# Two GpSimd products of each RWKV pair computed by VectorE, and the gate tile allocated from a longer-lived pool

## The chip, the cores and the metric

The kernel runs on one core of a Trainium2 chip. A core has five engines that run their own instruction queues side by side: TensorE (PE, matmuls; its weight loads are listed apart as PEld), VectorE (DVE), ScalarE (ACT), GpSimd (POOL) and SyncE (SP, which here only issues DMAs). They meet through semaphores: an instruction waits until the instructions that it depends on, on other engines or in DMA queues, have signalled. Within one engine the order is fixed, so an instruction that waits also holds up what stands behind it.

The metric is the device time of one launch in microseconds (us). The times shown are the median of several runs; the profile is of one execution.

## The reference

One layer of a hybrid trunk over 528 tokens (16 learned meta tokens ahead of 512), width 1024, all float32. Cut to what matters here:

```python
u = rmsnorm(h, norm_mix)
proj = u @ w_in                                     # 1024 -> RWKV, FoX and gate columns
gates = sigmoid(proj[..., C_RW + C_FX:] + b_gate)   # 2 x 1024 columns
y_rw = rwkv7_branch(...)                            # 8 heads of 64, delta rule over 64-token chunks
y_fx = fox_branch(...)                              # 8 heads, attention with forget gates
merged = gates[..., :1024] * (y_rw @ w_out_rw) + gates[..., 1024:] * (y_fx @ w_out_fx)
h = h + merged @ w_o
h = h + square(relu(rmsnorm(h) @ w_up)) @ w_down
```

In the RWKV branch, with `k`, `a`, `r` per head and `kk` the normalised key:

```python
k = k * (1.0 + (a - 1.0) * k_a)
y = wkv7_scan(r, decay, k, v, -kk, kk * a)
bonus = sum(r * k * r_k, axis=-1) * v
```

The changed products are two of these: `k` divided by the running decay of its chunk, and `r * k` for the bonus.

## The kernel before

Every float32 matrix product is made of three TensorE passes over a high and a low part (`hi`, `lo`) of each operand. For a weight block of 128x1024, SP loads two halves `wraw` of 128x512, ACT casts each to `whi` (L550), DVE subtracts to get `wlo` (L551), and PE runs `whi` with the high and low input and `wlo` with the high input (L582). In the later stages the same is done by `load_h` (L239 the load, L242 the casts).

The work goes through three stages:

- **Front** (0 to about 400 us): 40 projection blocks; the RWKV heads in four *pairs* (a pair is two heads side by side in the 128 partitions); the FoX attention; and the last 16 blocks, which are the gates. Pairs 0 and 1 form the first group, 2 and 3 the second; after a group's pairs come a triangular inverse and a chain over the 9 chunks of 64 tokens.
- **Merge** (about 400 to 460 us): eight rounds `m`. In each, two gate tiles `gl` come back from DRAM (L1261), ACT takes their tanh (L1262), PE makes two products `po` in PSUM banks with the tag `sm` (L1267, four banks, so two rounds), DVE multiplies gate and product (L1269), POOL adds the two (L1271), ACT and DVE write `mhi` and `mlo` (L1272, L1273). Then the product with `w_o`.
- **MLP** (to the end).

What sets the order. In the front, PE's order is written out by a planner: several generators run as streams, and `Turns.run` takes the stream of highest rank whose operands are ready by a clock of estimated times (`Clock.read`, L101 on, with `RATE` per engine). The other engines' orders are made by the framework's own scheduler from the program. In `Clock.read` an instruction is booked on the engine it runs on, except that `wlo` is booked as "Pool" (L116).

In a pair (`class Pair`) the steps that matter are these, all over 9 chunks of 64 columns (576, or 512 without the meta chunk):

- `keys`: from `okk` and the decay sum, PE makes the sums of squares `pkk`; L910 clamps them, ACT takes logarithm and exponential (L912, L913), L914 and L915 make the key `kp` (it lives in the tile `sg`), L916 normalises `okk`. Then L921 writes `KT`, L922 the first half of `BK`, **L923 the second half of `BK` as `kp3 * pinv` on POOL**, and L924 writes `KT` from all of `BK`.
- `rows`: L932, L933 and L935 on DVE write the tile `L` of the pair's first head, L934 and L938 on ACT copy its lower half to that of the second. **L939 writes `sq = orr * sg` on POOL**, the r·k product, which the PE product `pbn` of the bonus reads later.
- `scores`: in three rounds PE makes `psr` from `BK` and `L` (L964), DVE masks them into `Bm` and `L` (L965, L967), and PE transposes `KT` into `pbt` (L971). `psr` needs `BK` and both tiles `L`; `pbt` needs `KT`.

Between these, the same DVE queue carries the `wlo` subtractions (L551) and the token-shift evictions (L310: `orr`, `ov`, `okk`) of the projections, which PE also waits for; L636 and L638 make the forget gates, L225 and L1139 belong to the group norm and to the chain of chunks.

The 16 gate blocks go the way of `gate_job`: ACT evicts `pj` into `gt` (L595) and issues its store to the DRAM tile `gd` (L596) from its own queue. `gt` is one buffer of the pool `fp`, which lives for the front only; the tiles of the merge are taken from memory that the front's pools give back. The pool `wp`, with the weight tiles, is opened at L202 and lives through the whole kernel. Before the merge's first two rounds nothing but buffers holds the loads `gl` back: the gates `gd` 0, 1, 8 and 9 are in DRAM long before.

Of the kernel before, what the change touches and what calls it, by code (L numbers as in the profile page):

```python
# [9 lines left out]
F32 = mybir.dt.float32  # L10
# [4 lines left out]
ALU = mybir.AluOpType  # L15
# [6 lines left out]
S = 512  # L22
# [40 lines left out]
class Clock:  # L63
# [6 lines left out]
    def __init__(self, nc):  # L70
        self.nc = nc
        self.seen = len(nc.cur_bb.bb.instructions)
        self.pe = 0.0
        self.form = None
        self.urgent = False
        self.spans, self.w, self.r, self.free, self.rings = {}, {}, {}, {}, {}

    def last(self, name):
# [20 lines left out]
    def read(self):  # L99

        new = self.nc.cur_bb.bb.instructions[self.seen:]  # L101
        self.seen += len(new)
        for x in new:
            outs = [o.bass_ap for o in x.outs if hasattr(o, "bass_ap")]
            ins = [o.bass_ap for o in x.ins if hasattr(o, "bass_ap")]
            if not outs:
                continue
            for o in outs:
                t = o.tensor
                if hasattr(t, "cap_key") and t.name not in self.free:  # L110
                    ring, n = self.rings.setdefault(str(t.cap_key).rsplit("_", 2)[0], []), t.tag_meta.bufs
                    self.free[t.name] = self.last(ring[-n]) if len(ring) >= n else 0.0
                    ring.append(t.name)
            names = [a.tensor.name for a in ins]
            out = outs[0].tensor.name
            eng = "Pool" if out.startswith("wlo") else str(x.engine).split(".")[-1]  # L116

            def cols(a):
                return math.prod(n for _, n in a.ap[1:])
            deps = max([self.w.get(n, 0.0) for n in names] + [self.free.get(out, 0.0)])  # L120
            if eng == "PE":
                n = cols(outs[0])
                rows, width = x.tile_size
                if ins[0].dtype == F32R:
                    cost = n / 2400 + 0.013
                else:
                    cost = n / 600 * max(rows * width / 16384, 1 / 4)
                if self.form != tuple(x.tile_size):
                    self.form = tuple(x.tile_size)
                    cost += 0.1  # L130
                self.pe = end = max(self.pe, deps) + cost
            else:
                size = max([cols(a) for a in outs + (ins if "Reduce" in str(x.opcode) else [])])
                if eng in self.RATE and "DMA" not in str(x.opcode):
                    fixed, per = self.RATE[eng]
                    if eng == "DVE" and (getattr(x, "is_tensor_tensor_scan", False) or any(a.ap[-1][0] > 4 for a in outs + (ins[:1] if "Transpose" in str(x.opcode) else []))):
                        per *= 2
                    end = self.book(eng, max(deps, self.last(out)), fixed + per * size) + fixed + per * size
                else:
                    cost = 0.3 + size * 128 * 4 / 2.0e5  # L140
                    end = self.book("DMA", max(deps, self.last(out)), cost) + cost + 2.0
            for o in outs:
                self.w[o.tensor.name] = max(self.w.get(o.tensor.name, 0.0), end + self.HOP)
            for n in names:
                self.r[n] = max(self.r.get(n, 0.0), end + self.HOP)
# [44 lines left out]
def kernel(ctx, tc, ht, x, win, par, cst, gain, lora, wout, wo, wup, wdn, out, dbg=None):  # L190
# [4 lines left out]
    V, G, A = nc.vector, nc.gpsimd, nc.scalar  # L195
# [6 lines left out]
    wp = ctx.enter_context(tc.tile_pool(name="wp", bufs=2))  # L202
# [50 lines left out]
    def after(ins, prev):  # L253

        tc.add_manual_dep(ins.ins, prev.ins.name, mybir.DependencyInfo(mybir.DependencyClass.NoSync, mybir.DependencyReason.DATA),
                          reason="one accumulation at a time")
# [8 lines left out]
    def pinned(prev):  # L265

        if table["tanh"] or table["pin"] is None:
            p = nc.scalar.preload_act_table_set("natural_log_exp_and_others")
            after(p, prev)
            for x in table["tanh"]:  # L270
                after(p, x)
            table["tanh"], table["pin"] = [], p
        return table["pin"]
# [14 lines left out]
    with ExitStack() as st:  # L288
# [5 lines left out]
        def psm(name="psm"):  # L294
            return ps.tile([128, 512], F32, name=name, tag="sm", bufs=4)
# [22 lines left out]
        ck = Clock(nc)  # L318
# [180 lines left out]
        fp = st.enter_context(tc.tile_pool(name="fp", bufs=1))  # L499
# [7 lines left out]
        def banks(n):  # L507
            return ck.ring("sm", n, 4)
# [82 lines left out]
        def gate_job(i):  # L591
            def begin():
                def evac(po, sl):
                    gt = fp.tile([128, S], F32, name="gt")
                    act(gt, po, AF.Identity, bias=pr[:, C_BG + i:C_BG + i + 1])  # L595
                    A.dma_start(gates_d[i], gt)  # L596
                return evac
            return begin
# [226 lines left out]
        def v9(t):  # L825
            return t.rearrange("p (a b) -> p a b", b=64)
# [28 lines left out]
        class Pair:  # L855
# [44 lines left out]
            def keys(self):  # L900

                p = self.p
                okr, thr, kp, pinv = self.okk[:, PADT:], self.tha[:, PADT:], self.sg, v9(self.lc)
                self.sq = sq = rp.tile([128, TP], F32, name="sq")
                s_ = act(sq[:, :T], okr, AF.Square, scale=self.col(C_KK))
                yield lambda: max(ck.ready(sq), banks(2))
                for hc in (slice(0, HT), slice(HT, T)):
                    pq = psm("pkk")[:, :HT]
                    mm(pq, ones_blk, sq[:, hc], start=True, stop=True)
                    V.tensor_scalar(sq[:, hc], pq, 1e-24, None, ALU.max)  # L910
                pin = pinned(s_)
                after(act(sq[:, :T], sq[:, :T], AF.Ln), pin)  # L912
                act(sq[:, :T], sq[:, :T], AF.Exp, scale=-0.5)  # L913
                V.tensor_scalar(kp[:, PADT:], thr, prh[:, 2, p:p + 1], prh[:, 3, p:p + 1], ALU.mult, ALU.add)  # L914
                V.tensor_tensor(kp[:, PADT:], kp[:, PADT:], okr, ALU.mult)  # L915
                V.scalar_tensor_tensor(okr, okr, self.col(C_KK), sq[:, :T], ALU.mult, ALU.mult)  # L916
                kkn, kp3, tha3 = v9(self.okk), v9(kp), v9(self.tha)

                self.BK = BK = rp.tile([128, NCH, 2, 64], F32, name="BK", tag="BK")
                self.KT = KT = rp.tile([128, NCH, 2, 64], F32, name="KT", tag="KT")  # L920
                V.scalar_tensor_tensor(KT[:, :, 1, :], kkn, 0.5, pinv, ALU.mult, ALU.mult)  # L921
                V.scalar_tensor_tensor(BK[:, :, 0, :], tha3, 1.0, KT[:, :, 1, :], ALU.add, ALU.mult)  # L922
                G.tensor_tensor(BK[:, :, 1, :], kp3, pinv, ALU.mult)  # L923
                s_ = V.tensor_tensor(KT, BK, self.P[:, :, 63:64].unsqueeze(2).to_broadcast([128, NCH, 2, 64]), ALU.mult)  # L924
                if p == 0:
                    after(s_, low[0])

            def rows(self):

                kkn, r3, P = v9(self.okk), v9(self.orr), self.P  # L930
                self.L = l0, l1 = [kp.tile([128, NCH, 128], F32, name=f"L{e}", bufs=2) for e in range(2)]
                V.scalar_tensor_tensor(l0[:, :, 1:64], kkn[:, :, 1:64], -1.0, P[:, :, 0:63], ALU.mult, ALU.mult)  # L932
                V.tensor_scalar(l0[:, :, 0:1], kkn[:, :, 0:1], -1.0, None, ALU.mult)  # L933
                A.copy(l1[hss[1], :, :64], l0[hss[1], :, :64])  # L934
                s_ = V.tensor_tensor(l0[:, :, 64:128], r3, P, ALU.mult)  # L935
                if self.p == 0:
                    after(s_, low[0])
                A.copy(l1[hss[1], :, 64:], l0[hss[1], :, 64:])  # L938
                G.tensor_tensor(self.sq[:, :S], self.orr[:, 64:], self.sg[:, 64:], ALU.mult)  # L939
                self.rkb = rp.tile([128, 128], F32, name="rkb")  # L940
                after(V.tensor_scalar(self.rkb, ones_blk, self.col(C_RK), None, ALU.mult), last["DVE"])

# [673 lines left out]
```

## Time and profile before

| | |
|---|---|
| median of 3 runs | 826.9 us (826.32 to 827.44) |
| the profiled execution's own time | 826.71 us |
| its span in the trace | 824.9 us |
| mean granted TensorE clock | 0.998 |
| DVE busy | 607.8 us, 1196 instructions |
| ACT busy | 452.5 us, 941 instructions |
| POOL busy | 120.0 us, 124 instructions |
| POOL, L923 | 4 products 128x576, 1407, 1568 and 1801 ns (min, median, max) |
| POOL, L939 | 4 products 128x512, 1677, 1764 and 2303 ns |

The span is what the trace covers; the execution's own time has 1.8 us more around it. Times inside the trace are counted from the span's start. A row of a timeline gives start, duration, engine, line, operation, tiles and, in brackets, how long the engine was idle before it and what ended the wait. A row "x2" holds two instructions that followed one another. The four pairs run their L923 at 43, 74, 165 and 235 us and their L939 at 48, 81, 182 and 247 us.

### The profile page before, as it was taken

To read this page: it belongs to the slowest core of one execution; us is meant where nothing else is said; L and a number is where in the kernel's file an instruction comes from. 1 tells how busy PE (TensorE), PEld (TensorE's weight loads), DVE (VectorE), ACT (ScalarE), POOL (GpSimd) and SP (SyncE) were. 2 spreads that over 40 slices of the span, in tenths; PEclk is the share of its full clock that TensorE was granted. 3 is DMA by queue.
4 is the path that set the end of the run, shared out by engine and by line. 5 is a ranking of instruction groups with operands and counts; after the bars stand their busy time and mean duration, and the time that the engine had idled before them with its cause. 6 is when DMAs were issued, how large, how long until landed. Compare 5 with 4: busy or idle time off the path is not lost.

```text
span 824.9 us, 15506 instructions
## 1 busy us (share of the span) xinstructions
PE 808.1 (98%) x5886; PEld 667.3 (81%) x5886; DVE 607.8 (74%) x1196; ACT 452.5 (55%) x941; POOL 120.0 (15%) x124
## 2 busy tenths in 40 slices
PE   8999999998999999999999999999999999999998
PEld 6979887876987886778788889888888888888886
DVE  6797985687779855975267655875698678867988
ACT  7767548766575457664366534664445434543452
POOL 1021000010011000000022003100740174017400
PEclk9999999999999999999999999999999999999999
DMA  7222221211211311223687404533742365236532
GB/s 240 75 71 79 69 92 56 79 40 65 79 52 54 128 46 61 90 66 116 218 289 226 159 0 151 176 82 100 225 150 87 115 221 150 77 118 208 156 107 76
DMA packets 51483, 95.88 MB, mean 116 GB/s; under 512 B 5832, under 2 KB 7240, under 8 KB 51408
## 3 DMA queue, kind: packets, MB, share of 16 engines
q1 hardware_dynamic: 47680, 86.37, 33.0%
q0 software_dynamic: 1280, 4.20, 1.7%
q10 hardware_dynamic: 2448, 4.33, 1.5%
q8 instruction: 46, 0.75, 0.4%
q14 instruction: 29, 0.24, 0.1%
HBM read 88.56 MB, written 6.31 MB: 115 GB/s over the span
## 4 chain that ended last, share of the span: by engine, by line
PE 86%; DVE 5%; ACT 5%; issue 2%; DMA 1%; POOL 0%; DVEq 0%; ACTq 0%; SPq 0%
PE pj L582 22%; PE po L1357 21%; PE po L1484 12%; PE pd L1484 5%; PE po L1267 4%; PE po L1329 3%; PE pj L394 1%; PE pd L1298 1%; PE po L1298 1%; PE psc L751 1%; PE py L805 1%; PE psr L964 1%; PE ppt L788 1%; DVE wlo L551 1%; PE pch L1115 1%
## 5 line engine op out<-in xcount | busy, mean ns | idle before, releaser
L582 PE MATMUL pj<-uhi,whi 128*128 128x264 f32 (+1 forms) x480 | 164.3, 342 | 0.0
L582 PE MATMUL pj<-uhi,wlo 128*128 128x264 f32 (+1 forms) x480 | 153.9, 321 | 1.8 <-DVE wlo L551 1.8
L582 PE MATMUL pj<-ulo,whi 128*128 128x264 f32 (+1 forms) x480 | 153.8, 320 | 0.0
L242 DVE TENSOR_TENSOR wlo<-wraw,whi 128x512 fp32r<-128x512 f32 x84 | 81.0, 973 | 36.8 <-ACT whi L242 36.8
L582 PEld LDWEIGHTS pj<-uhi,whi 128*128 128x128 f32 x480 | 90.7, 189 | 12.9 <-issue 4.4
L582 PEld LDWEIGHTS pj<-uhi,wlo 128*128 128x128 f32 x480 | 90.7, 189 | 8.8 <-DVE wlo L551 2.2
L582 PEld LDWEIGHTS pj<-ulo,whi 128*128 128x128 f32 x480 | 91.0, 190 | 6.7 <-issue 1.6
L1357 PE MATMUL po<-zhi,whi 128*128 128x512 f32 (+1 forms) x248 | 94.8, 382 | 0.0
L1357 PE MATMUL po<-zlo,whi 128*128 128x512 f32 (+1 forms) x248 | 94.8, 382 | 0.0
L1357 PE MATMUL po<-zhi,wlo 128*128 128x512 f32 (+1 forms) x248 | 94.8, 382 | 0.0
L242 ACT CAST whi<-wraw 128x512 fp32r<-128x512 f32 x84 | 51.4, 617 | 53.5 <-PE po L1357 20.3
L551 DVE TENSOR_TENSOR wlo<-wraw,whi 128x512 fp32r<-128x512 f32 x78 | 53.8, 699 | 23.5 <-ACT whi L550 22.6
L550 ACT CAST whi<-wraw 128x512 fp32r<-128x512 f32 x78 | 47.7, 617 | 42.4 <-PE pj L582 41.7
L276 ACT CAST whi<-t 128x512 fp32r<-128x512 f32 x64 | 39.9, 624 | 44.6 <-DVE wlo L276 27.2
L1406 POOL TENSOR_TENSOR t<-traw 128x512 f32<-128x512 f32 x24 | 38.4, 1622 | 173.6 <-DMA traw<-in_wdn 173.6
L1484 PE MATMUL po<-wlo,fhi 128*128 128x512 f32 (+1 forms) x164 | 63.4, 387 | 0.2
L1484 PE MATMUL po<-whi,flo 128*128 128x512 f32 (+1 forms) x164 | 62.8, 384 | 0.0
L1484 PE MATMUL po<-whi,fhi 128*128 128x512 f32 (+1 forms) x164 | 62.3, 384 | 0.0
L276 DVE TENSOR_TENSOR wlo<-t,whi 128x512 fp32r<-128x512 f32 x64 | 43.5, 689 | 24.3 <-ACT whi L276 24.0
L1373 ACT CAST fhi<-R 128x768 fp32r<-128x768 f32 (+1 forms) x32 | 30.2, 945 | 49.1 <-DVE R L1380 26.1
L1357 PEld LDWEIGHTS po<-zlo,whi 128*128 128x128 f32 x248 | 46.6, 188 | 9.1
L1357 PEld LDWEIGHTS po<-zhi,wlo 128*128 128x128 f32 x248 | 46.6, 188 | 9.0
(330 smaller groups left out, 1706.4 us busy)
## 6 DMA issues: line engine op xcount, KB each, us to landing
wraw<-in_win SPq DMA_DIRECT2D x84, 256.0 KB, 2.6
wraw<-in_wup SPq DMA_DIRECT2D x60, 256.0 KB, 3.1
wraw<-in_wdn SPq DMA_DIRECT2D x48, 256.0 KB, 2.7
traw<-in_wdn SPq DMA_DIRECT2D x48, 256.0 KB, 3.5
gd<-gt ACTq DMA_DIRECT2D x16, 256.0 KB, 2.2
wraw<-in_wout SPq DMA_DIRECT2D x16, 256.0 KB, 3.9
gl<-gd SPq DMA_DIRECT2D x16, 256.0 KB, 3.8
traw<-in_wdn POOLq DMA_DIRECT2D x16, 256.0 KB, 3.1
```

Of the source, the lines that this page charges most:

```text
L242: casts.append((A.copy(hi, raw), low.tensor_tensor(lo, raw, hi.bitcast(F32), ALU.subtract)))
L276: return A.copy(hi, x), V.tensor_tensor(lo, x, hi.bitcast(F32), ALU.subtract)
L550: after(A.copy(hi, raw), last["ACT"])
L551: low[0] = V.tensor_tensor(lo, raw, hi.bitcast(F32), ALU.subtract)
L582: mm(po, a, b[:, k, a0:a1], start=n == 0, stop=n == 23)
L1267: mm(po, a, ys[k][:, b, :], start=n == 0, stop=n == 11)
L1298: mm(pd[i], a[:, k, 128 * i:128 * i + 128], b, start=k == 0 and n == 0, stop=k == 7 and n == 2)
L1329: mm(po, a[:, k, 128 * i:128 * i + 128], b[:, k, :], start=n == 0, stop=n == 23)
L1357: mm(po[:, t0:t1], a, b[:, k, t0:t1], start=n == 0, stop=n == 23)
L1373: A.copy(fhi[:, j, a:b], R[:, a:b])
L1406: eng.tensor_tensor(t, sums[c, pair] if c in (T1, T2) else c, d, ALU.add)
L1484: mm(x[i][:, cols], a[:, k, left, 128 * rows:128 * rows + 128], c[:, cols], start=start and k == 0 and n == 0, stop=stop and k == n_pairs ...
```

## The change

Three edits. Two products of each pair move from POOL to DVE, eight instructions in all. A new set `aside` keeps their names, and the planner books them as "Pool" as before. The tile `gt` of the gates is taken from `wp` with one buffer, in place of `fp`. Below L76 every line number of the new kernel is one higher.

```diff
@@ class Clock: __init__
         self.urgent = False
+        self.aside = set()
@@ class Clock: read
-            eng = "Pool" if out.startswith("wlo") else str(x.engine).split(".")[-1]
+            eng = "Pool" if out.startswith("wlo") or x.name in self.aside else str(x.engine).split(".")[-1]
@@ gate_job
-                    gt = fp.tile([128, S], F32, name="gt")
+                    gt = wp.tile([128, S], F32, name="gt", bufs=1)
@@ class Pair: keys
-                G.tensor_tensor(BK[:, :, 1, :], kp3, pinv, ALU.mult)
+                ck.aside.add(V.tensor_tensor(BK[:, :, 1, :], kp3, pinv, ALU.mult).ins.name)
@@ class Pair: rows
-                G.tensor_tensor(self.sq[:, :S], self.orr[:, 64:], self.sg[:, 64:], ALU.mult)
+                ck.aside.add(V.tensor_tensor(self.sq[:, :S], self.orr[:, 64:], self.sg[:, 64:], ALU.mult).ins.name)
```

PE's order is the same in both kernels. On DVE the neighbourhood of each pair is ordered anew. In pair 0, DVE's queue before, from the product that follows L916 on:

```order
L932 SCALAR_TENSOR_TENSOR L_662<-okk,P 128x9x63
L933 TENSOR_SCALAR L_662<-okk 128x9
L921 SCALAR_TENSOR_TENSOR KT<-okk,lc 128x9x64
L310 SCALAR_TENSOR_TENSOR orr<-pj,pr_65,tm 128x264
L849 TENSOR_TENSOR lw_1903<-lraw,lw_1902 128x128
L922 SCALAR_TENSOR_TENSOR BK<-tha,KT 128x9x64
L310 SCALAR_TENSOR_TENSOR orr<-pj,pr_65,tm 128x264
L924 TENSOR_TENSOR KT<-BK,P 128x1152
L551 TENSOR_TENSOR wlo<-wraw,whi 128x512 x2
L935 TENSOR_TENSOR L_662<-orr,P 128x9x64
```

And now:

```order
L933 SCALAR_TENSOR_TENSOR L_662<-okk,P 128x9x63
L934 TENSOR_SCALAR L_662<-okk 128x9
L922 SCALAR_TENSOR_TENSOR KT<-okk,lc 128x9x64
L924 TENSOR_TENSOR BK<-sg,lc 128x9x64
L850 TENSOR_TENSOR lw_1903<-lraw,lw_1902 128x128
L923 SCALAR_TENSOR_TENSOR BK<-tha,KT 128x9x64
L311 SCALAR_TENSOR_TENSOR orr<-pj,pr_65,tm 128x264
L925 TENSOR_TENSOR KT<-BK,P 128x1152
L311 SCALAR_TENSOR_TENSOR orr<-pj,pr_65,tm 128x264
L552 TENSOR_TENSOR wlo<-wraw,whi 128x512
L940 TENSOR_TENSOR sq<-orr,sg 128x512
L552 TENSOR_TENSOR wlo<-wraw,whi 128x512
```

The product of L923 (L924 now) stands behind `KT`, that of L939 (L940 now) between the two `wlo`, and L935 (L936 now) behind them. In pair 1, DVE's queue now, from the key `sg` of L915 on:

```order
L916 TENSOR_TENSOR sg<-sg,okk 128x528
L307 MEMSET tm 128x1
L924 TENSOR_TENSOR BK<-sg,lc 128x9x64
L311 SCALAR_TENSOR_TENSOR orr<-pj,pr_65,tm 128x264
L637 SCALAR_TENSOR_TENSOR forget_432<-forget_431,forget_432 8x528
L552 TENSOR_TENSOR wlo<-wraw,whi 128x512
L911 TENSOR_SCALAR sq<-pkk 128x264 x2
L639 SCALAR_TENSOR_TENSOR forget_433<-forget_431,forget_432 8x528
```

Before, the two clamps of `pkk` (L910) stood behind the scan L638 (L639 now). Further on in pair 1, L939's product stands behind L933, and one `wlo` has moved ahead of L922. In pair 3 the order is the old one with L923's product far ahead and L939's behind L933.

At the end of the front, ACT's queue before, with the last two gate tiles `gt`, the weight casts of the merge and the first two rounds of `gl`:

```order
L242 CAST whi<-wraw 128x512 x2
L595 ACTIVATE gt<-pj,pr 128x512
L596 DMA gd_94<-gt 128x512
L242 CAST whi<-wraw 128x512 x2
L595 ACTIVATE gt<-pj,pr 128x512
L596 DMA gd_95<-gt 128x512
L242 CAST whi<-wraw 128x512 x2
L1262 ACT_TABLE_LOAD
L1262 ACTIVATE gl_5402<-gl_5402 128x512
L1262 ACTIVATE gl_5419<-gl_5419 128x512
L1262 ACTIVATE gl_5451<-gl_5451 128x512
L1262 ACTIVATE gl_5468<-gl_5468 128x512
```

And now:

```order
L243 CAST whi<-wraw 128x512
L1263 ACT_TABLE_LOAD
L1263 ACTIVATE gl_5402<-gl_5402 128x512
L1263 ACTIVATE gl_5419<-gl_5419 128x512
L596 ACTIVATE gt<-pj,pr 128x512
L243 CAST whi<-wraw 128x512
L597 DMA gd_94<-gt 128x512
L1263 ACTIVATE gl_5451<-gl_5451 128x512
L1263 ACTIVATE gl_5468<-gl_5468 128x512
L243 CAST whi<-wraw 128x512 x2
L596 ACTIVATE gt<-pj,pr 128x512
L597 DMA gd_95<-gt 128x512
```

The table load and the first four tanh have moved ahead of the last two gate tiles. On SP the four loads `gl` of the first two rounds have moved from behind eight `wout` loads and two `hres` loads to behind the third and the fourth `wout` load; the first of them no longer waits for the store of the last `gt`, only for the last group norm's `y_rw` and its operands.

## The prediction

> **What bounds the kernel now.** The page comes first: which engine is full.
>
> ```profile
> span 824.9 us, 15506 instructions
> PE 808.1 (98%) x5886; PEld 667.3 (81%) x5886; DVE 607.8 (74%) x1196; ACT 452.5 (55%) x941; POOL 120.0 (15%) x124
> ```
>
> PE is busy 808.1 of 824.9 us. The change takes no work from PE, so it can win only what PE now waits in the stages that it touches. Stretch by stage (length, then PE's busy time):
>
> ```profile
> 35.00:60.00 25.00, 23.20 (x217) 20.05 (x216) 21.80 (x40) 16.21 (x36) 4.80 (x7) 1.00 0.27 82
> 60.00:95.00 35.00, 33.49 (x303) 30.00 (x302) 29.54 (x52) 24.58 (x51) 5.29 (x8) 1.00 0.25 79
> 160.00:205.00 45.00, 42.61 (x400) 31.44 (x399) 36.38 (x115) 27.98 (x81) 3.81 (x7) 0.98 0.17 54
> 235.00:260.00 25.00, 23.61 (x223) 19.77 (x222) 20.46 (x34) 15.94 (x35) 4.33 (x4) 1.00 0.17 55
> 400.00:460.00 60.00, 58.97 (x260) 48.51 (x260) 35.13 (x53) 34.26 (x58) 11.64 (x8) 1.00 0.81 264
> ```
>
> Pairs 0 to 3 lie in the first four, the start of the merge in the fifth. PE idles 1.80, 1.51, 2.39, 1.39 and 1.03 us in them: 8.1 us is the ceiling. The waits of PE name who ends them (us in total, times, longest):
>
> ```profile
> PE pbt L971 <- DVE KT L924: 2.1, 2, 1.3
> PE pj L582 <- DVE wlo L551: 1.8, 1, 1.8
> PE psc L751 <- DVE nm L762: 1.5, 1, 1.5
> PE po L1267 <- DVE gl L1269: 1.0, 1, 1.0
> PE psr L964 <- DVE Bm L965: 0.4, 1, 0.4
> ```
>
> None names POOL, yet DVE is what PE waits for in pairs 0, 1 and 3 (`wlo`, `KT`, `Bm`). Why DVE is late there shows when its timeline is laid beside POOL's. Pair 0, POOL and then DVE:
>
> ```profile
> 43.49 1.80 POOL L923 TENSOR_TENSOR BK<-sg,lc 128x576 f32<-128x576 f32 x1 [8.02 <-ACT lc L896]
> 47.84 2.30 POOL L939 TENSOR_TENSOR sq<-orr,sg 128x512 f32<-128x512 f32 x1 [0.29 <-DVE orr L310]
> ...
> 43.93 1.40 DVE L933 TENSOR_SCALAR L<-okk 128x9 f32<-128x9 f32 x1
> 48.93 2.35 DVE L551 TENSOR_TENSOR wlo<-wraw,whi 128x512 fp32r<-128x512 f32 x2
> 51.21 0.75 DVE L935 TENSOR_TENSOR L<-orr,P 128x576 f32<-128x576 f32 x1
> ```
>
> Pairs 1 and 3, again POOL and then DVE:
>
> ```profile
> 73.86 1.41 POOL L923 TENSOR_TENSOR BK<-sg,lc 128x576 f32<-128x576 f32 x1 [21.71 <-DVE tm L306]
> 80.97 1.68 POOL L939 TENSOR_TENSOR sq<-orr,sg 128x512 f32<-128x512 f32 x1 [4.53 <-DVE okk L916]
> 247.46 1.78 POOL L939 TENSOR_TENSOR sq<-orr,sg 128x512 f32<-128x512 f32 x1 [10.97 <-DVE okk L916]
> ...
> 74.23 1.60 DVE L636 SCALAR_TENSOR_TENSOR forget<-forget,forget 8x528 f32<-8x528 f32 x1
> 81.41 1.84 DVE L932 SCALAR_TENSOR_TENSOR L<-okk,P 128x567 f32<-128x567 f32 x1
> 83.17 0.16 DVE L933 TENSOR_SCALAR L<-okk 128x9 f32<-128x9 f32 x1
> 248.02 1.26 DVE L933 TENSOR_SCALAR L<-okk 128x9 f32<-128x9 f32 x1
> ```
>
> L933, nine columns, takes 0.16 us at 83.17 but 1.40 at 43.93, until 45.33, and POOL's product ends at 45.29; at 248.02 it ends at 249.28, POOL's at 249.24. L932 takes 1.84 at 81.41, where L935 with as many columns takes 0.75: POOL ends at 82.65, and 0.6 later so does L932. **DVE stands still while a POOL product runs.** The bill: L933 1.24, the two `wlo` about 1.07 (2.35 against 1.28 for two elsewhere in pair 1), L636 about 1.05 (POOL ends at 75.27, of 1.60 only 0.55 lies behind it), L932 1.09, L933 1.10: 5.5 us.
>
> [...]
>
> **The change part by part.** Price of a product on DVE: no row shows L923 or L939 there. L935, 128x576 from two SBUF tiles, takes 0.75, and the next starts 0.68 later; a 128x512 `wlo` steps by 0.61. I take 0.67 and 0.63, bounds 0.6 (that step) and 0.8 (L935 with nothing overlapped). So 8 products cost 5.2 us of DVE and end 5.5 us of stalls: near balance, and the place decides.
>
> *Pair 0.* PE waits 1.80 us, 48.94 to 50.74, for the first `wlo` behind L939. Now from L932's end at about 43.95: L933 0.07, L921 0.67, L923 0.67, then L849 0.21, L922 0.67, the two `orr` 0.81 and L924 1.26 as today (their starts today are 0.3 to 1.3 apart), so `wlo` starts at 48.3 and ends near 49.0: wait gone. Then L939 0.63, the second `wlo` 0.65, L935 0.68 to 50.9, ACT's copy L938 of 0.67 to 51.65, and `psr` can start at 51.7. Today:
>
> ```profile
> 51.99 0.67 ACT L938 COPY L<-L 64x576 f32<-64x576 f32 x1 [2.64 <-DVE tm L306]
> 52.55 0.71 PE L964 MATMUL psr<-L,BK 64*64 64x128 f32 x12
> ```
>
> PE would be there at 50.8, so **a new wait of 0.85 on L938 takes the place of half the old one**. Gain 0.9; bounds 0.5 (products at 0.8) and 1.8 (all of the idle).
>
> *Pair 1.* Three waits: 0.28 for `BK`, 0.78 for `KT`, 0.45 for `Bm`.
>
> ```profile
> 78.47 0.65 ACT L912 ACTIVATE sq<-sq 128x528 f32<-128x528 f32 x1 [2.04 <-DVE sq L910]
> 84.03 0.76 DVE L922 SCALAR_TENSOR_TENSOR BK<-tha,KT 128x576 f32<-128x576 f32 x1
> 84.84 0.89 PE L964 MATMUL psr<-L,BK 64*64 64x128 f32 x24 [0.28 <-DVE BK L922]
> 86.51 0.55 PE L971 MATMUL pbt<-cs,KT 128*128 128x128 f32 x3 [0.78 <-DVE KT L924]
> ```
>
> ACT waits 2.04 us for the clamps L910, which now run ahead of the scan and not behind it. L923 adds 0.67 and L636's stall takes 1.05 off, so L910 stands at 75.95, 1.7 earlier, and ACT with it; the scan, one `wlo` and `orr` follow, and L916 starts near 78.95 in place of 80.05. From there L935, L932 (without 1.09), L933, L939 (+0.63), L921, a `wlo` moved ahead (+0.65) and L922, which ends near 83.8. PE arrives at 84.56: no wait. L924 ends near 85.5, PE arrives at 85.45, so 0.05 of 0.78 stays. The `wlo` that moved ahead no longer stands before `Bm`, ready near 87.1, as PE comes. Gain 1.35; bounds 0 (products at 0.8, L910 no earlier: then the stalls' 2.1 only pay for 1.6 and the moved `wlo`) and 1.5.
>
> *Pair 2.* Its products cost 1.3 on DVE, and one stall of 1.1 (L225) ends:
>
> ```profile
> 182.51 1.26 DVE L225 TENSOR_TENSOR rsgw<-st,rsgy 128x8 f32<-128x8 f32 x1
> ```
>
> What PE needs soonest there is the chain's `uv` (L1139):
>
> ```profile
> 177.07 0.58 DVE L1139 TENSOR_TENSOR uv<-pch,SP 64x128 f32<-64x128 f32 x2
> 178.74 0.45 PE L1109 MATMUL pch<-uv,L 128*64 128x64 f32 x8
> ```
>
> It ends 1.09 before its use, and in the new order the second product and two `pe` scalings stand near it: I put it at most 0.7 later, and 0.4 stays. PE's long wait in this stretch, 1.5 for `nm` at 201.9, comes 18 us after the last product. Gain 0, bounds ±0.5.
>
> *Pair 3.* PE waits 1.31 for `KT`:
>
> ```profile
> 251.96 1.35 DVE L924 TENSOR_TENSOR KT<-BK,P 128x1152 f32<-128x1152 f32 x1
> 253.46 0.52 PE L971 MATMUL pbt<-cs,KT 128*128 128x128 f32 x3 [1.31 <-DVE KT L924]
> ```
>
> L923 lies 12 us ahead in slack. From L933: 1.10 goes, L939's 0.63 comes; that is 0.47. ACT's copy L934, which waits for L933, starts 1.1 earlier, and behind it the cast that the second `wlo` waits for, so that DVE's short gap there closes too. Gain 0.65; bounds 0.3 and 1.3.
>
> *The gate's tile.* At the merge's start:
>
> ```profile
> SPq L1261 <- DMA gd<-gt: 4.4, 1, 4.4
> 389.80 0.42 DVE L1179 TENSOR_TENSOR y_rw<-yT,pg 128x256 f32<-128x256 f32 x1
> 409.43 1.28 ACT L1262 ACT_TABLE_LOAD   x1 [3.33 <-DMA gl<-gd]
> ```
>
> SP holds `gl` back until the last `gt` is stored; landing, table load and tanh then make DVE late, and PE, whose four `po` banks are full, waits 1.03 us for L1269. With `gt` elsewhere the first `gl` can be issued once the last `y_rw` is written, at 390.22, and the tanh lie near 396, over 6 us before the first `po` ends. PE's 1.03 go. The price is paid by what stands behind on ACT: the table load (1.28) and two tanh (1.15) hold up a `gt` and a weight cast by some 3 us, and that weight is wanted only about 5 us after. Gain 1.0; bounds 1.03 and -1.
>
> **Sum:** 0.9 + 1.35 + 0 + 0.65 + 1.0 = 3.9 us. The profiled execution took 826.71, so 822.8; the median of the runs stands 0.2 above it: **823.0**.
>
> **The rivals.**
>
> *Slower: the long DVE instructions are not POOL's doing.* If L933 and the others wait for something else that ends by chance with POOL's product, no stall goes, and the products lie on the path: pair 0 0.67 + 0.63, pair 1 the same, pair 3 0.63, in all 3.2 us, less 1.0 at the merge: +2.2, 829.1. It decides when less than a quarter of the 5.5 us goes (0.25 x 5.5, 0.7 of better order in pairs 1 and 3, and 1.0 at the merge make 3.1). Against it: five ends that coincide. For it: no trace without POOL. 1 in 12.
>
> *The wait moves on.* In each pair the next operand is as late as the one before: `psr` on L938 in pair 0 (gain 0.5), `KT` in pair 1 with the `wlo` now ahead of it (0.4), `KT` in pair 3 (0.3), and 1.0 at the merge: 2.2, 824.7. For it: pair 0 as I work it out loses half its gain that way, and in pair 1 `KT` has 0.05 to spare. 1 in 5.
>
> *Same: only the merge gains,* or only the pairs gain a little, since each us of the pairs comes back at pair 2's chain or a late `gl`: 0 to 1.5, about 826. For it: 5.2 us of new DVE work against 5.5 us. 3 in 20.
>
> **How the numbers follow.** The forecast, 3 to 5 us, has 0.57; the moved wait 0.20; same 0.15; slower 0.08. About 0.2%, 1.65 us, is what a measurement of this kernel can tell from no change. So faster 0.76, same 0.16, slower 0.08. The range takes in the forecast with its upper bounds (1.8 + 1.5 + 1.3 + 1.0 gives 821.3) and the moved wait: 821.2 to 825.6.
>
> **What would show it.** L933 at 0.16 and L932 at 0.75 in all four pairs; no idle of PE before the `wlo` of pair 0, but 0.85 before `psr` on L938; `pbt` of pair 1 with less than 0.2, of pair 3 with 0.6; no wait of L1267 for L1269; SP's `gl` issued near 390. Wrong I would be if L923 on DVE took over 0.9 us, if a wait on Rs L1111 or nm L762 grew in pair 2, or if weight casts late by the table load starved PE near 403.

## The result and the profile after

| | before | changed |
|---|---|---|
| median, first comparison (5 runs each) | 826.32 us (824.23 to 827.44) | 822.13 us (820.53 to 823.79) |
| ratio to before | | 0.9947, 95% interval 0.9927 to 0.9967 |
| median, second comparison (17 and 5 runs) | 826.72 us (824.0 to 828.48) | 822.07 us (820.9 to 823.23) |
| ratio to before | | 0.9941, interval 0.9926 to 0.9956 |
| profiled execution, its span | 826.71, 824.9 us | 820.67, 818.9 us |

The changed kernel is 0.5 to 0.6% faster, 4 to 5 us. The page of its profile, and PE's stretches with the same columns as before (length, busy time of PE, PEld, DVE, ACT and POOL, granted clock, DMA share, GB/s):

```profile
span 818.9 us, 15502 instructions
PE 807.3 (99%) x5886; PEld 666.9 (81%) x5886; DVE 601.6 (73%) x1204; ACT 453.5 (55%) x941; POOL 107.2 (13%) x116
```

```profile
35.00:60.00 25.00, 24.64 (x225) 21.11 (x224) 21.69 (x45) 17.18 (x38) 0.69 (x5) 1.00 0.26 82
60.00:95.00 35.00, 34.96 (x317) 31.74 (x316) 30.29 (x56) 25.34 (x53) 2.20 (x6) 1.00 0.25 80
160.00:205.00 45.00, 42.60 (x398) 31.74 (x397) 37.67 (x122) 28.67 (x80) 0.80 (x6) 1.00 0.17 52
235.00:260.00 25.00, 24.26 (x223) 21.12 (x223) 20.86 (x37) 16.38 (x35) 1.24 (x2) 1.00 0.14 44
400.00:460.00 60.00, 60.00 (x266) 49.71 (x265) 39.36 (x60) 32.72 (x58) 11.52 (x8) 1.00 0.70 233
```

PE's idle time in the stretch of pair 0 goes from 1.80 to 0.36, of pair 1 from 1.51 to 0.04, of pair 3 from 1.39 to 0.74, at the merge from 1.03 to 0; that of pair 2 stays at 2.4. DVE makes eight instructions more and is busy 6.2 us *less*; in the changed kernel's second profile it is 2.8 less (605.0), since DVE's rows in later stages differ from one execution to the next. In the pairs alone the rows that were long before are some 7.7 us shorter together, and the eight products add 5.7 by their rows: the work that came is smaller than the standing still that went. PE's waits by who ends them, without the two of the kernel's start:

```profile
PE pch L1116 <- DVE Rs L1112: 1.8, 3, 1.2
PE psc L752 <- DVE nm L763: 1.5, 1, 1.5
PE pbt L972 <- DVE KT L925: 0.7, 1, 0.7
PE py L1144 <- ACT y_rw L1096: 0.6, 1, 0.6
PE psr L965 <- ACT L L939: 0.3, 1, 0.3
```

The rows on `wlo`, `Bm`, `BK` and `gl` are gone; a small one on ACT's copy (L939 now, L938 before) is new. The DVE rows that were long before, in pairs 0, 1 and 3, and PE's and ACT's at the new wait:

```profile
44.32 0.17 DVE L934 TENSOR_SCALAR L<-okk 128x9 f32<-128x9 f32 x1
48.68 0.68 DVE L552 TENSOR_TENSOR wlo<-wraw,whi 128x512 fp32r<-128x512 f32 x1
74.00 0.69 DVE L637 SCALAR_TENSOR_TENSOR forget<-forget,forget 8x528 f32<-8x528 f32 x1
79.40 0.73 DVE L933 SCALAR_TENSOR_TENSOR L<-okk,P 128x567 f32<-128x567 f32 x1
244.14 0.17 DVE L934 TENSOR_SCALAR L<-okk 128x9 f32<-128x9 f32 x1
...
51.27 0.67 ACT L939 COPY L<-L 64x576 f32<-64x576 f32 x1 [1.10 <-DVE tm L307]
51.29 0.43 PE L965 MATMUL psr<-L,BK 64*64 64x128 f32 x2
51.99 0.88 PE L965 MATMUL psr<-L,BK 64*64 64x128 f32 x22 [0.27 <-ACT L L939]
```

All five are short now, 0.17 for the nine columns, 0.73 for 567. Two of `psr`'s matmuls run at 51.29, while ACT's copy, begun at 51.27, is not done; only the third waits for it.

PE runs the same instructions in the same order in both kernels, so the n-th matmul of one trace can be set against the n-th of the other, and each change of their distance is time won or lost at that place. In the profile of the second comparison (`e0_again`), which like that of before has one stretch of half clock at the same place (last section), against before:

| place | step of the distance | forecast |
|---|---|---|
| first `wlo` of pair 0 | -1.71 | |
| `psr` of pair 0 | +0.61 | |
| pair 0 in all | **-1.10** | -0.9 |
| `BK`, `KT` and `Bm` of pair 1 (0.35 + 0.75 + 0.61) | **-1.71** | -1.35 |
| pair 2 | 0 | 0 |
| `psr` and `KT` of pair 3 (0.15 + 0.57) | **-0.72** | -0.65 |
| L1267 at the merge's start | **-1.32** | -1.0 |

The sum is -4.9. The start of the kernel, before anything changed, lay 0.4 later, and the rest came 0.1 earlier, which makes the 4.6 us between the spans of 824.9 and 820.3. An ended wait pays about its idle row, and in some places more: 1.71 for 1.80, 0.35 for 0.28, 0.61 for 0.45, 1.32 for 1.03. A wait's row gives only the time in which nothing of PE shows.

### The profile page after: what moved, and what is told of

The parts are those of the page before. It is cut to its first block, busy times and chain, and to the rows that moved or that the text cites. A ratio compares the mean times of both kernels' runs of the same rounds, so it can differ in the third digit from the quotient of the medians.

```text
span 818.9 us, 15502 instructions
## 1 busy us (share of the span) xinstructions
PE 807.3 (99%) x5886; PEld 666.9 (81%) x5886; DVE 601.6 (73%) x1204; ACT 453.5 (55%) x941; POOL 107.2 (13%) x116
## 4 chain that ended last, share of the span: by engine, by line
PE 91%; DVE 4%; ACT 3%; issue 1%; DVEq 0%; ACTq 0%
PE pj L583 25%; PE po L1358 21%; PE po L1485 12%; PE po L1268 5%; PE pd L1485 5%; PE po L1330 3%; PE pj L395 1%; PE pd L1299 1%; PE po L1299 1%; PE psc L752 1%; PE py L806 1%; PE psr L965 1%; PE ppt L789 1%; PE pch L1116 1%; PE pch L1110 1%
```

## The experiments

### One edit at a time: the gate's tile

```diff
-                    gt = fp.tile([128, S], F32, name="gt")
+                    gt = wp.tile([128, S], F32, name="gt", bufs=1)
```

> The gate's tile alone, products left on POOL. If the merge's start gives its 1.0 by itself: the wait of L1267 for L1269 (1.03 us) is gone, the gl loads are issued over 10 us earlier against PE's gate blocks than before, the waits in pairs 0, 1 and 3 stand as before (1.80, 1.51 and 1.31), and the time falls by 1.0 to 1.3 us, ratio 0.9985. Rival, the merge's wait ended only because the products left POOL and let the front run differently: the wait of 1.0 stays and the time does not change.

Measured: 826.93 us median of 11 runs against 826.72, ratio 0.9997, interval 0.9986 to 1.0008. PE's wait at the merge is gone, and those in the pairs stand (1.80, 1.30). In this profile against that of before the merge's start gives a step of 1.32, yet the runs show 0.3 at the most likely, 1.2 at the most. The size was missed.

### The products without the gate's tile

The changed kernel with `gt` in `fp` again.

> The eight products on DVE, the gate's tile as before. If the POOL products held DVE: L933 takes 0.17 and no longer 1.4, the waits in pairs 0, 1 and 3 shrink by 1.2, 1.7 and 0.6 us (3.5 in all), that of L1267 stays at 1.0, and the time falls by 3 to 3.6 us, ratio 0.996. Rival, most of the measured fall came with the gate's tile or with a fuller clock: the fall is under 1.5 us.

Measured: 822.71 us median against 826.72, ratio 0.9947, interval 0.9933 to 0.9962: 4.4 us, most of the 4.9 that the changed kernel shows against the same runs of before. The pairs' steps are 1.11, 1.70 and 0.71, the 3.5 that were expected. But PE's wait at the merge was not the 1.03 that it should have kept:

```profile
408.07 0.73 PE L1268 MATMUL po<-ys,whi 128*128 128x512 f32 x2 [0.39 <-DVE gl L1270]
```

### Both once more, for the merge

The kernel before and the products alone were profiled a second time, unchanged.

> The kernel before once more, for its profile. If the wait of L1267 for L1269 at the merge's start hangs on when the gl loads land: it lies somewhere between 0 and 1.1 us and need not be 1.03, while the waits in pairs 0, 1 and 3 come out within 0.1 us as in the first profile (1.80, 1.51, 1.31). Rival, it is set by the program's order: 1.0 again.

> The products alone once more, the gate's tile as before. By the landing: a wait of L1267 for L1269 between 0 and 1.1 us, another than the first time's 0.39. Rival, the program's order sets it: 0.39 again.

Measured: the waits in the pairs of `b_again` are 1.80, 0.26 + 0.78 + 0.45 and 1.31, as in the first profile. **At the merge neither of the two has a row of PE waiting.** By PE's steps 0.5 us are still lost there in `b_again` and 0.3 in `e2_again`, against 1.3 in the first profile of before. The row on SP's wait for the last `gt`, 4.4 us in the first profile, in `b_again`:

```profile
SPq L1261 <- DMA gd<-gt: 2.5, 1, 2.5
```

SP waited 1.9 us less for the store of `gt`. That alone does not set PE's wait: with the BK product alone on DVE (next section) SP waits 2.6 and PE 0.95, with the r·k product alone 3.0 and 0. The loads `gl` behind it land late or soon as well. What counts is both: from the issue of the last store to the table load, which waits for the first `gl`, 8.15 us pass in the first profile of before and 7.27 in `b_again`, here in this order:

```profile
401.28 0.33 ACTq L596 DMA_DIRECT2D gd<-gt  x1
409.43 1.28 ACT L1262 ACT_TABLE_LOAD   x1 [3.33 <-DMA gl<-gd]
...
402.77 0.33 ACTq L596 DMA_DIRECT2D gd<-gt  x1
410.04 1.28 ACT L1262 ACT_TABLE_LOAD   x1 [2.45 <-DMA gl<-gd]
```

There are seven profiles with `gt` in `fp`: before twice, the products alone twice, and the three runs below that keep it there. In them PE waits 1.03, 0.95 and 0.39 where this stretch takes 8.15, 8.07 and 7.51, and has no row where it takes 7.27 or less. The mean is 0.34 by the rows and 0.6 by PE's steps; over the profiles with `gt` in `wp` PE never waits there. So the edit does what was said, and what it is worth is the mean of a wait that is often not there. It agrees with the 0.3 (at most 1.2) of the runs with that edit alone.

### The BK product alone, and the r·k product alone

The kernel before, with one of the two products on DVE and booked as Pool, the other on POOL, `gt` in `fp`.

> Only the BK product (L923) on DVE; the r*k product (L939) stays on POOL, the gate's tile as before. If each POOL product holds DVE at its own place: L933 of pair 0 falls from 1.40 to 0.17 and L636 from 1.60 to 0.6, but the wlo of pair 0 (2.35 for two), L932 of pair 1 (1.84) and L933 of pair 3 (1.26) stay long; PE waits about 1 us for wlo or psr in pair 0 and 1.3 for KT in pair 3. Rival, the long instructions have another cause: none of the five shortens by itself.

> Only the r*k product (L939) on DVE; the BK product stays on POOL. If each POOL product holds DVE at its own place: L933 of pair 0 and L636 stay at 1.3 to 1.6, L932 of pair 1 takes 0.75 and L933 of pair 3 0.17; pair 3's wait for KT falls to about 0.7, pair 0's wait for wlo is gone or under 0.6. Rival: as in the run before.

With L923 alone on DVE (its lines, one higher), POOL still making the r·k product at 48.66 to 50.32 and 247.34 to 249.12:

```profile
44.13 0.17 DVE L934 TENSOR_SCALAR L<-okk 128x9 f32<-128x9 f32 x1
48.50 2.38 DVE L552 TENSOR_TENSOR wlo<-wraw,whi 128x512 fp32r<-128x512 f32 x2
74.38 0.68 DVE L637 SCALAR_TENSOR_TENSOR forget<-forget,forget 8x528 f32<-8x528 f32 x1
247.90 1.26 DVE L934 TENSOR_SCALAR L<-okk 128x9 f32<-128x9 f32 x1
```

With L939 alone on DVE, POOL still making the BK product at 43.59 to 45.39 and 73.44 to 74.86:

```profile
44.03 1.40 DVE L934 TENSOR_SCALAR L<-okk 128x9 f32<-128x9 f32 x1
73.80 1.61 DVE L637 SCALAR_TENSOR_TENSOR forget<-forget,forget 8x528 f32<-8x528 f32 x1
80.97 0.74 DVE L933 SCALAR_TENSOR_TENSOR L<-okk,P 128x567 f32<-128x567 f32 x1
245.79 0.17 DVE L934 TENSOR_SCALAR L<-okk 128x9 f32<-128x9 f32 x1
```

Each product that stays on POOL holds DVE while it runs, and the long rows of the other are gone. PE's waits follow: with the BK product alone on DVE 0.48 + 0.27 at pair 0's `psr` and 1.30 for `KT` in pair 3, with the r·k product alone 0.40 for `BK` and 0.78 for `KT` in pair 1 and 0.74 for `KT` in pair 3. By PE's steps the BK product alone wins 0.6, 1.3 and 0 us in pairs 0, 1 and 3, the r·k product alone 0.5, 0.5 and 0.7. The times, 828.26 and 822.26 us beside 825.81 for the kernel before, are of one run each and tell nothing. Two lines of the expectations failed. With the BK product alone, L932 of pair 1 was to stay long and took 0.73: there POOL's product was late itself, and the row that it held is another (last section). With the r·k product alone, PE still waits for pair 0's `wlo`, and long:

```profile
50.37 0.50 PE L583 MATMUL pj<-uhi,wlo 128*128 128x512 f32 x1 [1.33 <-DVE wlo L552]
```

L934 is still held for 1.2 there, and DVE's r·k product now stands ahead of the `wlo`: the hold has ended, and DVE's own work has come in its place.

### The product made a second time on POOL

```diff
+                G.tensor_tensor(self.sq[:, :S], self.orr[:, 64:], self.sg[:, 64:], ALU.mult)
```

behind DVE's own, into the same tile.

> As the changed kernel, but POOL makes the r*k product a second time behind DVE's, into the same tile; nothing on DVE waits for it. If a POOL product that reads SBUF holds DVE: in each pair an instruction of DVE behind it takes about 1.1 us too long and ends with POOL's product, and pair 3's wait of pbt for KT grows from 0.74 to about 1.5. Rival, dependencies: nothing waits for it but the bonus, so DVE's durations and PE's waits stay as in the changed kernel.

POOL's second product of pair 3, what stands behind it on DVE, and PE:

```profile
247.35 1.65 POOL L941 TENSOR_TENSOR sq<-orr,sg 128x512 f32<-128x512 f32 x1 [17.08 <-ACT L L935]
...
247.76 1.78 DVE L552 TENSOR_TENSOR wlo<-wraw,whi 128x512 fp32r<-128x512 f32 x1
...
250.26 0.89 PE L966 MATMUL psr<-L,BK 64*64 64x128 f32 x24 [0.69 <-DVE BK L923]
252.23 0.52 PE L973 MATMUL pbt<-cs,KT 128*128 128x128 f32 x3 [1.08 <-DVE KT L925]
```

A `wlo` that takes 0.68 elsewhere takes 1.78: it ends at 249.54, 0.54 behind POOL's end at 249.00, and PE waits 1.77 in pair 3 in place of 0.74. Pair 1 has a `wlo` of 1.58, pair 2 an L226 of 1.10 for 0.16. None of these three waits for a signal of POOL. What holds DVE is that POOL runs the product, not that anything depends on it. By PE's steps it takes back 1.0 us of the gain in pair 1 and 1.1 in pair 3. Only in pair 0 DVE lost no more than 0.3: there POOL's product took 2.26 us where those of pairs 1 and 3 took 1.65, beside a DVE that issued without a gap at its usual lengths (0.75 for L936, 0.48 for each `ov`).

### A constant in place of the r·k product

```diff
-                G.tensor_tensor(self.sq[:, :S], self.orr[:, 64:], self.sg[:, 64:], ALU.mult)
+                G.memset(self.sq[:, :S], 0.5)
```

> As the kernel before, but in place of the r*k product POOL fills its tile with a constant (the bonus term is left out of the result so). If it is POOL's reading of SBUF that holds DVE: with a POOL memset of the same size L932 of pair 1 takes 0.75, L933 of pair 3 0.17 and the two wlo of pair 0 1.28, L933 of pair 0 (the BK product) still 1.4; pair 3's wait for KT falls to about 0.1. Rival, any POOL work at that place holds DVE: these stay long for as long as the memset runs, about 0.5 us.

Pair 3, POOL and then DVE:

```profile
248.37 0.53 POOL L939 MEMSET sq<- 128x512 f32 x1 [10.95 <-DVE okk L916]
...
248.28 0.75 DVE L932 SCALAR_TENSOR_TENSOR L<-okk,P 128x567 f32<-128x567 f32 x1
248.95 0.17 DVE L933 TENSOR_SCALAR L<-okk 128x9 f32<-128x9 f32 x1
```

POOL fills the tile while L932 reads two tiles, and neither is slower for it (0.75, and 0.53 as in the other three pairs). In pair 0 the fill runs early, at 43.67, again beside an L932 of 0.75, and in pair 1 beside an L935 of 0.75. L932 of pair 1 (0.74) and pair 0's two `wlo` (1.28) are short too, with no POOL product beside them, and L933 of pair 0, beside the BK product, still takes 1.40. So not everything that POOL runs holds DVE: an L932 that began 0.06 behind the start of a fill took 0.75 (pair 0 here), one that began 0.44 behind the start of a product 1.84 (pair 1, before). That the product *reads* two tiles and the fill none would fit; no run shows it apart from the rest in which the two differ. L933, a nine-column row that reads one tile, is held by a product as well (1.40 for 0.17). The waits went differently in two places: 0.36 for `KT` in pair 3 where 0.1 was expected, and in pair 0 a new one of 2.19 for `KT`, since on DVE's queue, with the fill in place of the product, L924 now stands behind both `ov` and four `wlo`.

### The planner's booking

```diff
-            eng = "Pool" if out.startswith("wlo") or x.name in self.aside else str(x.engine).split(".")[-1]
+            eng = "Pool" if out.startswith("wlo") else str(x.engine).split(".")[-1]
```

> The changed kernel, but the planner books the eight products on DVE, where they run, and not as Pool. If the booking only keeps PE's order: PE's order changes at the pairs, some waits move, and the time is within 1 us of the changed kernel (ratio to before 0.993 to 0.996). Rival, the order that the Pool booking keeps is what the gain rests on: over 1.5 us of it go, ratio above 0.996.

Measured: 825.41 us median of 12 runs against 827.03, ratio 0.9986, interval 0.9976 to 0.9996. **Without the booking some three quarters of the gain are lost**: 1.2 us of 4.4 to 4.9 are left, 0.3 to 2.0 by the interval. The first theory failed. PE's order changes, and in pair 1 the sums of squares are put ahead of projections that were there to cover them:

```profile
74.40 1.16 PE L910 MATMUL pkk<-sq,cs 128*128 128x264 f32 x4 [3.34 <-ACT sq L906]
```

One wait of 3.34 us, for ACT, takes the place of nearly all that pairs 0, 1 and 3 had won (3.5 by the table). Which price in the planner moved this step stays open.

### The r·k product later

The changed kernel, with the r·k product of pairs 0 and 3 made behind the first round of scores:

```diff
-                ck.aside.add(V.tensor_tensor(self.sq[:, :S], ...).ins.name)
+                if self.p in (1, 2):
+                    ck.aside.add(V.tensor_tensor(self.sq[:, :S], ...).ins.name)
@@ def scores, behind the masks of a round
+                    if c0 == 0 and self.p in (0, 3):
+                        sq = V.tensor_tensor(self.sq[:, :S], ...)
+                        ck.aside.add(sq.ins.name)
+                        after(sq, s_)
```

> As the changed kernel, but in pairs 0 and 3 the r*k product is put behind the first round of scores. If its place on DVE's queue is what is left of the waits: pair 0's wait of psr for the copy L938 (0.6 us of delay) and about 0.6 of pair 3's 0.74 for KT go, and the time falls by about 1.2 us against the changed kernel, ratio to before 0.993. Rival, the wait moves on to the masks L965 of the next round: PE's idle time in pairs 0 and 3 stays above 0.7 us in all and the time is that of the changed kernel.

> The changed kernel once more, beside the others on one chip. If its gain is 4.6 us at full clock: ratio 0.994 to 0.996, and PE idles 0.3 in pair 0, 0 in pair 1, 0.74 in pair 3 and 0 at the merge's start, as in its first profile. Rival, the profile of before was a low one: another share of the gain, under 3 us.

Measured together: 821.38 us (ratio 0.9937, interval 0.9920 to 0.9954) and, for the changed kernel, 822.07 (0.9941, 0.9926 to 0.9956). PE's wait for ACT's copy in pair 0 is gone, and of pair 3's is left:

```profile
249.50 0.52 PE L977 MATMUL pbt<-cs,KT 128*128 128x128 f32 x3 [0.36 <-DVE KT L925]
```

The waits that ended make about 1.0 us by PE's steps (0.6 in pair 0, 0.4 in pair 3), a little less than the 1.2 expected. In pair 3 some 0.3 of it is lost again at the `psr` of the next rounds, as the rival said; what is left, 0.7, is what the medians differ by. It is the fastest kernel measured, but the intervals overlap so far that it can't be called faster than the changed one.

## Why the prediction was right, point by point

- **DVE stands still while a POOL product runs**: shown in the pairs. Each product left on POOL keeps long rows beside it (1.40 and 1.61 beside the BK product, 2.38 for two `wlo` and 1.26 beside the r·k product), and a product that nothing held by it waits for brings long rows back as well (1.58 and 1.78 for a `wlo` of 0.68). It does not hold throughout: beside one product of 3.08 us four DVE instructions ran at their usual length (last section). The rival that something else made the rows long is out. The bill of 5.5 us left out two rows, L225 of pair 2, which the prediction shows further on, and L898 of pair 3 (1.39 for 0.17): with them it is some 7.7, so that the balance was better than "near".
- **The products' price on DVE**, 0.67 and 0.63: the rows are 0.75 and 0.68 long, with the next starting 0.68 and 0.60 later.
- **Pair 0**, 0.9 forecast, 1.10 measured. The new wait on the copy came as said (it ends at 51.99, forecast 51.7, with the kernel's start 0.4 later in this profile), but it costs 0.6 and not 0.85: less that start, PE came to `psr` 0.1 later than worked out and the copy ended 0.1 earlier, and the first two matmuls did not wait for it.
- **Pair 1**, 1.35 forecast, 1.71 measured. All three waits went. L910 ahead of the scan did what was worked out: L916 starts at 78.05, where 78.95 was forecast, since all of it lies 0.7 earlier by then. The three ended waits pay 1.71 where their rows add up to 1.51.
- **Pair 2**, 0 forecast and 0 measured. **Pair 3**, 0.65 forecast and 0.72 measured; 0.74 of its wait is left, 0.6 forecast.
- **The gate's tile**, 1.0 forecast: the mechanism is right, the size is not. `gl` is issued at 385.74 and the table load runs at 388.58, ahead of the last two gate tiles, and nothing starves behind it. But the 1.03 was read from one profile. The second profile of the same kernel has no such row, the mean over seven is 0.34 by the rows and 0.6 by PE's steps, and the runs with this edit alone show 0.3, at most 1.2. This is the term of the sum that was mis-sized. It went unseen in the total because the pairs gave 0.6 more than forecast: that the median of 822.1 lies so near the 823.0 is in part luck.
- **The booking** had no term at all: the prediction took PE's unchanged order as given. Without it 3 to 4 of the 4 to 5 us are lost.

The rival "the wait moves on" was right for pair 0, in part, and nowhere else.

## What to carry to other kernels

When a small VectorE instruction takes many times what its twin takes elsewhere (1.40 us for 0.16 here), lay GpSimd's timeline beside it: an end that coincides to a few hundredths (0.04 here, twice) points to the one that holds it, a run with that product moved shows it, and then GpSimd work is not free even where GpSimd is as little busy as here (15% of the span). A wait that hangs on when a DMA lands should be read from several profiles before it is priced (here 1.03, 0.95 and 0.39 us in three of seven, no row in four), while the pairs' waits between engines repeated to within 0.05 us here. Where a planner writes the order, keep the order and the move of work apart, and measure both.

## What was not expected of the hardware

A POOL product took longer too, beside several DVE instructions that followed one another without a gap. With the BK product alone on DVE, POOL's r·k product of pair 1 took 3.08 us where its other three took 1.66 to 1.78, while four DVE instructions beside it ran at their usual length (three of them here) and the next long one was held in its turn, until 0.62 behind POOL's end:

```profile
79.32 3.08 POOL L940 TENSOR_TENSOR sq<-orr,sg 128x512 f32<-128x512 f32 x1 [3.67 <-DVE okk L917]
...
79.78 0.73 DVE L933 SCALAR_TENSOR_TENSOR L<-okk,P 128x567 f32<-128x567 f32 x1
80.43 0.16 DVE L934 TENSOR_SCALAR L<-okk 128x9 f32<-128x9 f32 x1
80.51 0.74 DVE L922 SCALAR_TENSOR_TENSOR KT<-okk,lc 128x576 f32<-128x576 f32 x1
81.28 1.74 DVE L923 SCALAR_TENSOR_TENSOR BK<-tha,KT 128x576 f32<-128x576 f32 x1
```

The granted clock fell to half, 0.50, for stretches of 3.4 us. Nine of the thirteen profiles have one such stretch at 200 to 205 us into the span, two have one of twice the length there, two none (their mean clocks are 1.000 and 0.999); in before's profile:

```profile
203.00:204.00 1.00, 1.00 (x17) 0.85 (x16) 0.94 (x3) 0.00 (x0) 0.00 (x0) 0.58 0.00 0
204.00:205.00 1.00, 1.00 (x9) 0.88 (x6) 1.00 (x4) 0.66 (x2) 0.14 (x1) 0.50 0.00 0
```

By PE's steps such a stretch costs about 1.4 us. The first profile of the changed kernel has none, which is why its span is 6.0 us shorter and not 4.6; the runs of one kernel spread over 2 to 5 us, in good part with their mean clock, from 824.0 at 1.00 to 828.48 at 0.996 for the kernel before.
